# Storing the last output tiles by column halves, and the last matrix products by output block, in an encoder layer

## The chip, the cores and the metric

The kernel runs on one core of a Trainium2 chip. The metric is device time in microseconds (us). Before the change it was 1040.94 us, the median of three runs (1040.69 to 1042.45).

## The reference

One encoder layer on a 512 x 1024 float32 residual stream: a half SwiGLU step, two attention mixers with gates, and a second half SwiGLU step. Only the end of the last step bears on this change:

```python
def swiglu(h, w_in, w_out):
    gate, up = jnp.split(h @ w_in, 2, axis=-1)
    return (jax.nn.silu(gate) * up) @ w_out
...
        h = modulate(rmsnorm(x, norm_ffn2[l]), sh3, sc3)
        x = x + 0.5 * g3[:, None, :] * swiglu(h, w_ffn2_in[l], w_ffn2_out[l])
    return x
```

The returned `x` is what the kernel stores: 512 x 1024 float32, 2 MB.

## The kernel before

The stream is held transposed in eight SBUF tiles `x[0]` to `x[7]`, each 128 channels by 512 tokens (256 KB). In what follows a *row block* of the result is one such tile; its halves `T1` and `T2` are its first and last 256 tokens (`HALVES`). In DRAM the output has the same layout, `(8, 128, 512)`, so a whole tile is 128 rows of 2 KB, and one half is 128 rows of 1 KB that lie 2 KB apart.

**Units.** The second SwiGLU step is cut into units (class `Unit`), each of which makes a 2 x 2 block product with seven sub-products instead of eight. The sub-products have names: `a11`, `a12`, `s1`, `s2`, `s3`, `s4`, `a22`. An outgoing unit (`out_unit(part, g, final)`) multiplies part of `w_ffn2_out` by the activations; `g` is 0 or 1 and stands for the upper or lower four row blocks. The last two outgoing units, `end[0]` and `end[1]`, have `final=True` and `depth` 3: the operand has three slices `k` = 0, 1, 2.

**A sub-product.** `Unit.multiply(q, ks)` picks the PSUM bank and calls `two` for each `k`. A bank is 128 x 512: columns 0 to 255 are output block `j` = 0, columns 256 to 511 are block `j` = 1. For one `k`, `two` runs both blocks, and for each block three matmuls (float32 is done as high times high, high times low, low times high; lines L456, L457, L458). So a sub-product of an end unit is 3 slices x 2 blocks x 3 = 18 matmuls.

**After a sub-product.** `Unit.after(q)` adds partial results on VectorE and calls `post` when one corner of the 2 x 2 block is complete. Corner `c11` is complete after `a12`, `c22` after `s3`, `c12` after `s4` and `c21` after `a22`. In `post`, corner `c(n)(t)` updates the token half `t` of two row blocks, with one scalar-tensor-tensor instruction each (L1810): 128 x 256, `x = v * g3 + x`. The first reads columns 0 to 255 of the result, the second columns 256 to 511. For `c21`, `v` is the PSUM bank itself; for the others it is an SBUF tile.

**Stores.** In `final` units, `post` counts the updates of each tile in `seen` and stores the whole tile from SyncE's queue (SP) after its second one (L1813): tiles 0, 1, 4, 5 after `c12`, tiles 2, 3, 6, 7 after `c21`.

**Order.** The sub-products of all units stand in a list (`items`) that sets the order on TensorE. Its end is `a12`, `s2`, `s3`, `s4`, `a22`, each for `end[0]` and then for `end[1]`, so the very last 18 matmuls are `a22` of `end[1]`, into a bank of the pool `sc`; the 18 ahead of them are `a22` of `end[0]`, into a bank of `acc`. While the end units run, GpSimd's DMA queue (POOL, L511) still fetches parts of `w_ffn2_out` with an add in flight, from which the weights of `s2`, `s3` and `s4` come; these are split into high and low parts on ScalarE and VectorE (L189). SP issues its last load at about 1009 us of the span.

Of the kernel before, what the change touches and what calls it, by code (L numbers as in the profile page):

```python
# [133 lines left out]
def layer(ctx: ExitStack, tc: tile.TileContext, a: dict):  # L134
    nc = tc.nc
# [12 lines left out]
    def xt():  # L148
        return sbuf("x", [P, T], F32, 8)
# [13 lines left out]
    def bank(tag):  # L163
        return psum.tile([P, T], F32, name=name(tag), tag=tag, bufs={"acc": 3, "op": 1, "sc": 3, "tp": 1}[tag])
# [41 lines left out]
    def let_go(holder):  # L206
        for i in [i for i in holders if holders[i] == holder]:
            del holders[i]

    def load_split(src, n=1024, spare=False, aside=0):  # L210
        raw = sbuf("raw", [P, 1024], F32, RAW)
        if spare:
            hi, lo = (u4().rearrange("p a b -> p (a b)") for _ in range(2))
        else:
            hi, lo = high_low(aside=aside)
        nc.sync.dma_start(raw[:, 0:n], src)
        split_from(hi[:, 0:n], lo[:, 0:n], raw[:, 0:n])
        return hi, lo

    HALVES = (slice(0, 2 * P), slice(2 * P, T))  # L220
# [12 lines left out]
    x = [xt() for _ in range(NC)]  # L233
# [199 lines left out]
    def pair_banks():  # L433
        return (bank("acc"), bank("sc"))
# [11 lines left out]
    OPERAND = {"a11": "b11", "s1": "n1", "a12": "b21", "a22": "t4", "s4": "b22", "s2": "n2", "s3": "t3"}  # L446
    BANK = {"a11": "x", "s2": "x", "s3": "x", "a22": "x", "s1": "v", "s4": "v", "a12": "w"}
    T1, T2 = HALVES

    def two(po, w, k, x, first, last):  # L450

        (wh, wl), (xh, xl) = w, x
        for j in range(2):
            s = slice((2 * k + j) * P, (2 * k + j + 1) * P)
            out = po[:, j * H : (j + 1) * H]
            PE.matmul(out, wh[:, s], xh, start=first and j == 0, stop=False, skip_group_check=True)  # L456
            PE.matmul(out, wh[:, s], xl, start=False, stop=False, skip_group_check=True)  # L457
            PE.matmul(out, wl[:, s], xh, start=False, stop=last and j == 1, skip_group_check=True)  # L458

    class Unit:  # L460
# [12 lines left out]
        MAKE = {"s1": 5, "a11": 3, "a12": 2, "s2": 4, "s4": 2, "s3": 2, "a22": 3}  # L473
        asked, length = ("s1", "a11", "a12", "a22"), 1.0

        in_order = turned = ()
        spare, roomy, apart, more = ("s1",), (), (), {"s1": ("s2", "a11"), "s2": ("s4", "a12"), "a11": ("s3", "a21")}

        def place(self, q):
# [34 lines left out]
        def multiply(self, q, ks=None):  # L514
            b = BANK[q]
            ks = range(self.depth) if ks is None else ks
            if b not in self.bank:
                self.bank[b] = bank(self.tags.get(b) or ("sc" if self.odd else "acc"))
            po = self.bank[b]
            new = not any(BANK[d] == b for d in self.done)  # L520
            for k in ks:
                x = self.operand(OPERAND[q], k)
                two(po, self.ready[q], k, x, new and k == 0, k == self.depth - 1)
            if self.depth - 1 in ks:
                let_go((self, q))

# [96 lines left out]
    with tc.manual_schedule(engines=BOUND | {mybir.EngineType.SP, mybir.EngineType.Pool}):  # L623
# [15 lines left out]
        for n in range(NC):  # L639
            i, j = n // 4, n % 4  # L640
# [329 lines left out]
    with tc.manual_schedule(engines={mybir.EngineType.SP, mybir.EngineType.Pool}):  # L970
# [4 lines left out]
        for q in range(4, 2 * PLAIN):  # L975

            w, sums_from = loaded1, split[1]
# [4 lines left out]
            out = pair_banks()  # L982
# [14 lines left out]
        for n, chunks in enumerate(CHUNKS):  # L997


            final = n + 1 == len(CHUNKS)  # L1000
# [20 lines left out]
            out = Out1(chunks, "acc" if nxt.odd != final else "sc", final)  # L1021
            if final:
                first = range(len(chunks) - 2)
# [52 lines left out]
    for i in range(2):  # L1076
        o = ROW_LAM + 2 * i * HD
        V.tensor_tensor_reduce(
            out=lam_p[:, i, :], in0=row[:, o : o + HD], in1=row[:, o + HD : o + 2 * HD],
# [439 lines left out]
    def start_a():  # L1519
        order = [(g, i) for i in range(2) for g in range(2)]  # L1520
        ys, v = [f2() for _ in order], f2()
        nc.sync.dma_start(ys[0], qa_scr[order[0]])
        nc.sync.dma_start(v, va_scr.rearrange("p t c -> p (t c)"))
        for y, o in zip(ys[1:], order[1:]):
            banded_last[:] = [nc.sync.dma_start(y, qa_scr[o]).ins]
        mask = u4(F32).rearrange("p a b -> p (a b)")[:, 0 : 3 * P]
        nc.sync.dma_start(mask, a["mask"])
        vz = b8()
        two = [vz[:, 2 * i : 2 * i + 2, :].rearrange("p a b -> p (a b)") for i in range(2)]
        two = [v.rearrange("p (t k w d) -> p t k w d", t=NT, k=2, w=2) for v in two]  # L1530
        zero = small(1)
        V.memset(zero, 0.0)
        v4 = v.rearrange("p (t k d) -> p t k d", t=NT, k=2)
        for kv in range(2):
            for t in two:
                V.tensor_copy(t[:, :, kv, 1 - kv, :], zero.unsqueeze(1).broadcast_to([P, NT, HD]))
            split_from(*(t[:, :, kv, kv, :] for t in two), v4[:, :, kv, :])
        wa.update(mask=mask, v=two, q=(b8(), b8()), o=(b8(), b8()))
        for n, ((g, i), y) in enumerate(zip(order, ys)):
            line.at(line.now + FETCH + n, lambda g=g, i=i, y=y: turn_queries_a(g, i, y), ("tp",))  # L1540
# [178 lines left out]
    x = [xt() for _ in range(NC)]  # L1719
# [3 lines left out]
    last = []  # L1723
# [4 lines left out]
    for m in range(NC):  # L1728
        w = load_split(a["w_mix"][m], aside=MIX_ASIDES[m])
# [70 lines left out]
            yield  # L1800

    def out_unit(part, g, final):
        seen = {}

        def post(c, v, u):
            n, t = int(c[1]) - 1, int(c[2]) - 1
            for j in range(2):
                m = 4 * g + 2 * n + j
                xr = x[m][:, HALVES[t]]
                V.scalar_tensor_tensor(xr, v[:, j * H : (j + 1) * H], modv[G3][:, m : m + 1], xr, ALU.mult, ALU.add)  # L1810
                seen[m] = seen.get(m, 0) + 1
                if final and seen[m] == 2:
                    nc.sync.dma_start(a["out"][m], x[m])  # L1813

        r = slice(part.start * 2 * P, part.stop * 2 * P)
        srcs = {q: a["w2o"][g, i][:, r] for i, q in enumerate(("a11", "a12", "a21", "a22"))}
        return Unit(srcs, len(part), act_operand, post, g)
# [88 lines left out]
    with tc.manual_schedule(engines=BOUND):  # L1906
# [7 lines left out]
        for m, products in last:  # L1914
            po = bank("sc")[:, 0:H]
            run(products(po, T1))
            update(m, po, T1)
        for i, (m, products) in enumerate(last):
            po = bank("sc")[:, 0:H]
# [86 lines left out]
    for i, part in enumerate(PARTS):  # L2006
        for p in list(part)[(3 if i == 0 else 1):] + list(range(part.stop, min(part.stop + 1, NH))):
            seq.append((units[p], p - 1))
        if part.stop < NH:
            seq += [(out_unit(part, g, False), None) for g in range(2)]  # L2010

    end = [out_unit(PARTS[-1], g, True) for g in range(2)]
    for v in end:
        v.in_order = ("s4",)
    for v, p in seq:
        item(v, "s1", rest=p is None)
        item(u, "a22")
# [83 lines left out]
```

## Time and profile before

| what | value |
|---|---|
| median of the runs shown | 1040.94 us |
| span of the profiled execution, first to last instruction | 1039.1 us |
| TensorE busy (its ends are modelled) | 1031.4 us, 99% of the span |
| VectorE busy | 787.7 us, 76% |
| ScalarE busy | 583.8 us, 56% |
| granted TensorE clock, mean | 0.999 |
| share of the chain that ended last on TensorE | 94% |
| stores of the result | 8 of 256 KB, median 2.3 us from issue to landing |

The profile gives the profiled execution by its span alone; its own device time is not listed. The median of the runs shown lies 1.9 us above the span. That rest, ahead of the first and behind the last instruction, is taken as unchanged wherever a span is turned into a time.

How to read it: TensorE is busy through nearly the whole span at nearly the full clock, and the stretches without it are the start and what lies behind the last matmul. The change touches the last two units; their rows are those of the last 30 us.

### The profile page before, as it was taken

How to read it: one execution, taken by the hardware profiler on the slowest of the kernel's cores; microseconds unless marked ns; L12 is line 12 of the kernel's file. 1: busy time of each engine (PE TensorE's matmuls, PEld its weight loads, DVE VectorE, ACT ScalarE, POOL GpSimd, SP SyncE). 2: the span in 40 equal slices, each digit the busy share in tenths (PEclk: the TensorE clock that was granted, in tenths of full speed). 3: DMA queues.
4: the chain of work that ended last, by engine and by line, in shares of the span. 5: the costliest groups of instructions: out<-in, count | busy, mean ns of one | idle time of the engine just before them, and what ended most of it. 6: DMA issues, size and time to landing. Idle time of an engine off the chain costs nothing.

```text
span 1039.1 us, 18835 instructions
## 1 busy us (share of the span) xinstructions
PE 1031.4 (99%) x7346; PEld 952.4 (92%) x7346; DVE 787.7 (76%) x1456; ACT 583.8 (56%) x1014; POOL 162.9 (16%) x190
## 2 busy tenths in 40 slices
PE   9999999999999999999999999999999999999998
PEld 7789899899998998899888888989999999999998
DVE  7786667567796679859772588976899777877867
ACT  6665335244465343667785856525867546655553
POOL 1101110110110100543333101001112112212210
PEclk9999999999999999999999999999999999999999
DMA  9978787967884359796737944974498998989974
GB/s 363 358 233 203 234 231 212 257 160 221 237 203 138 146 201 410 234 286 138 182 71 190 263 129 158 359 248 102 97 237 193 246 225 207 230 221 216 206 149 112
DMA packets 69225, 220.92 MB, mean 213 GB/s; under 512 B 8336, under 2 KB 11024, under 8 KB 69136
## 3 DMA queue, kind: packets, MB, share of 16 engines
q1 hardware_dynamic: 46656, 146.52, 38.8%
q0 software_dynamic: 19344, 68.70, 36.3%
q10 hardware_dynamic: 3136, 4.51, 1.2%
q8 instruction: 57, 0.93, 0.3%
q14 instruction: 32, 0.26, 0.1%
HBM read 209.46 MB, written 10.23 MB: 211 GB/s over the span
## 4 chain that ended last, share of the span: by engine, by line
PE 94%; DMA 2%; DVE 2%; ACT 2%; issue 0%; SPq 0%; DVEq 0%; ACTq 0%
PE acc L457 7%; PE acc L456 7%; PE acc L458 7%; PE sc L456 6%; PE sc L457 6%; PE sc L458 6%; PE sc L173 5%; PE sc L174 5%; PE sc L175 5%; PE acc L173 5%; PE acc L175 5%; PE acc L174 5%; PE tp L1269 2%; DMA raw<-w1s 2%; PE acc L1193 2%; PE acc L1191 2%
## 5 line engine op out<-in xcount | busy, mean ns | idle before, releaser
L189 ACT CAST high<-raw 128x1024 fp32r<-128x1024 f32 (+2 forms) x176 | 158.4, 913 | 150.7 <-PE sc L174 41.1
L189 DVE TENSOR_TENSOR low<-raw,high 128x1024 fp32r<-128x1024 f32 (+2 forms) x176 | 183.5, 1052 | 40.2 <-ACT high L189 38.7
L456 PE MATMUL acc<-b,high 128*128 128x256 f32 x508 | 140.9, 277 | 0.0
L457 PE MATMUL acc<-b,high 128*128 128x256 f32 x508 | 140.8, 277 | 0.1
L458 PE MATMUL acc<-b,low 128*128 128x256 f32 x508 | 140.6, 277 | 0.0
L457 PE MATMUL sc<-b,high 128*128 128x256 f32 x500 | 138.2, 276 | 0.0
L456 PE MATMUL sc<-b,high 128*128 128x256 f32 x500 | 138.2, 276 | 0.0
L458 PE MATMUL sc<-b,low 128*128 128x256 f32 x500 | 138.2, 276 | 0.0
L189 ACT CAST high<-u 128x1024 fp32r<-128x1024 f32 (+1 forms) x73 | 75.5, 1035 | 52.6 <-PE sc L174 20.2
L189 DVE TENSOR_TENSOR low<-u,high 128x1024 fp32r<-128x1024 f32 (+1 forms) x73 | 87.7, 1202 | 21.3 <-ACT high L189 19.6
L173 PE MATMUL sc<-b,high 128*128 128x512 f32 (+1 forms) x272 | 97.5, 358 | 0.0
L174 PE MATMUL sc<-b,high 128*128 128x512 f32 (+1 forms) x272 | 97.1, 357 | 0.0
L175 PE MATMUL sc<-b,low 128*128 128x512 f32 (+1 forms) x272 | 97.1, 357 | 0.0
L457 PEld LDWEIGHTS acc<-b,high 128*128 128x128 f32 x508 | 95.5, 188 | 0.4 <-DVE b L1885 0.3
L456 PEld LDWEIGHTS acc<-b,high 128*128 128x128 f32 x508 | 95.5, 188 | 0.3 <-ACT f L533 0.2
L458 PEld LDWEIGHTS acc<-b,low 128*128 128x128 f32 x508 | 95.4, 188 | 0.0
L456 PEld LDWEIGHTS sc<-b,high 128*128 128x128 f32 x500 | 93.9, 188 | 0.0
L458 PEld LDWEIGHTS sc<-b,low 128*128 128x128 f32 x500 | 93.9, 188 | 0.0
L457 PEld LDWEIGHTS sc<-b,high 128*128 128x128 f32 x500 | 93.9, 188 | 0.0
L173 PE MATMUL acc<-b,high 128*128 128x512 f32 (+1 forms) x240 | 89.0, 371 | 0.0
L175 PE MATMUL acc<-b,low 128*128 128x512 f32 (+1 forms) x240 | 86.7, 361 | 0.0
L174 PE MATMUL acc<-b,high 128*128 128x512 f32 (+1 forms) x240 | 86.6, 361 | 0.0
(397 smaller groups left out, 2720.6 us busy)
## 6 DMA issues: line engine op xcount, KB each, us to landing
u<-w_mod SPq DMA_DIRECT2D x38, 512.0 KB, 8.1
b<-w_mod SPq DMA_DIRECT2D x32, 512.0 KB, 5.7
raw<-w2i SPq DMA_DIRECT2D x31, 512.0 KB, 5.4
u<-w2i POOLq DMA_DIRECT2D x31, 512.0 KB, 7.4
raw<-w1u SPq DMA_DIRECT2D x24, 512.0 KB, 6.4
u<-w1u POOLq DMA_DIRECT2D x24, 512.0 KB, 6.6
raw<-w1o SPq DMA_DIRECT2D x24, 384.0 KB, 4.9
raw<-w_gate SPq DMA_DIRECT2D x16, 512.0 KB, 5.4
```

Of the source, the lines that this page charges most:

```text
L173: PE.matmul(out, wh, xh, start=first, stop=False)
L174: PE.matmul(out, wh, xl, start=False, stop=False)
L175: PE.matmul(out, wl, xh, start=False, stop=last)
L189: last = S.copy(hi, src), V.tensor_tensor(lo, src, f(hi), ALU.subtract)
L456: PE.matmul(out, wh[:, s], xh, start=first and j == 0, stop=False, skip_group_check=True)
L457: PE.matmul(out, wh[:, s], xl, start=False, stop=False, skip_group_check=True)
L458: PE.matmul(out, wl[:, s], xh, start=False, stop=last and j == 1, skip_group_check=True)
L1191: PE.matmul(out[t][:, 0:n], hh[k][:, ht], wh[:, o : o + n], start=k == 0, stop=False)
L1193: PE.matmul(out[t][:, 0:n], hl[k][:, ht], wh[:, o : o + n], start=False, stop=k == NC - 1)
L1269: PE.transpose(tp[:, j * P : (j + 1) * P], src, ident)
```

## The change

It has two parts. (1) In a final unit each half of a tile is stored as soon as its update has been issued, in place of the whole tile after both: sixteen stores of 128 KB (128 rows of 1 KB) for eight of 256 KB. (2) In the end units the sub-product `a22` goes block by block: all three slices for columns 0 to 255, then all three for columns 256 to 511. The matmuls are the same in number and form.

```diff
-    def two(po, w, k, x, first, last):
+    def two(po, w, k, x, first, last, js=range(2)):
...
-        for j in range(2):
+        for j in js:
...
-            for k in ks:
-                x = self.operand(OPERAND[q], k)
-                two(po, self.ready[q], k, x, new and k == 0, k == self.depth - 1)
+            for js in ((0,), (1,)) if q in self.by_columns else (range(2),):
+                for k in ks:
+                    x = self.operand(OPERAND[q], k)
+                    two(po, self.ready[q], k, x, new and k == 0, k == self.depth - 1, js)
...
-        seen = {}
...
-                seen[m] = seen.get(m, 0) + 1
-                if final and seen[m] == 2:
-                    nc.sync.dma_start(a["out"][m], x[m])
+                if final:
+                    nc.sync.dma_start(a["out"][m][:, HALVES[t]], xr)
...
-        v.in_order = ("s4",)
+        v.in_order, v.by_columns = ("s4",), ("a22",)
```

In SP's queue, these are the last rows before the change: the whole tiles, named `x_872` (tile 0) to `x_879` (tile 7).

```order
L1813 DMA out<-x_872_7096 128x512 [waits DVE_49]
L1813 DMA out<-x_873_7097 128x512 [waits DMAHW1_49,DVE_49]
L1813 DMA out<-x_876_7100 128x512 [waits DMAHW2_49,DVE_49]
L1813 DMA out<-x_877_7101 128x512 [waits DMAHW3_49,DVE_49]
L1813 DMA out<-x_874_7098 128x512 [waits DVE_49]
L1813 DMA out<-x_875_7099 128x512 [waits DMAHW5_49,DVE_49]
L1813 DMA out<-x_878_7102 128x512 [waits DMAHW6_49,DMASW6_49,DVE_49]
L1813 DMA out<-x_879_7103 128x512 [waits DMAHW7_49,DVE_49]
```

With the change there are sixteen; these are the ninth to the last, the stores after `c12` and `c21`.

```order
L1811 DMA out<-x_872_7096 128x256 [waits DMAHW0_49,DVE_49]
L1811 DMA out<-x_873_7097 128x256 [waits DMAHW1_49,DVE_49]
L1811 DMA out<-x_876_7100 128x256 [waits DMAHW2_49,DVE_49]
L1811 DMA out<-x_877_7101 128x256 [waits DMAHW3_49,DVE_49]
L1811 DMA out<-x_874_7098 128x256 [waits DMAHW4_49,DVE_49]
L1811 DMA out<-x_875_7099 128x256 [waits DMAHW5_49,DVE_49]
L1811 DMA out<-x_878_7102 128x256 [waits DMAHW6_49,DVE_49]
L1811 DMA out<-x_879_7103 128x256 [waits DMAHW7_49,DVE_49]
```

The eight of the same tiles after `c11` and `c22` stand ahead of them in the same order, so half of the bytes has moved forward to the earlier updates. Each row waits for VectorE's update, and by DMAHW0 to DMAHW7 for the landing of an earlier transfer on the same of eight completion counters; for these eight rows that is the store eight places ahead.

On TensorE, these are the last nine matmuls before the change, in the `a22` of `end[1]`. The bank is `sc_1129`, and `b8_1106`, `b8_1120` and `b8_1133` hold the operand's slices `k` = 0, 1 and 2.

```order
L456 MATMUL sc_1129_11050<-b8_1120_10963,high_86 128x256
L457 MATMUL sc_1129_11050<-b8_1120_10963,high_86 128x256
L458 MATMUL sc_1129_11050<-b8_1120_10963,low_93 128x256
L456 MATMUL sc_1129_11050<-b8_1133_11106,high_86 128x256
L457 MATMUL sc_1129_11050<-b8_1133_11106,high_86 128x256
L458 MATMUL sc_1129_11050<-b8_1133_11106,low_93 128x256
L456 MATMUL sc_1129_11050<-b8_1133_11106,high_86 128x256
L457 MATMUL sc_1129_11050<-b8_1133_11106,high_86 128x256
L458 MATMUL sc_1129_11050<-b8_1133_11106,low_93 128x256
```

And these are the last nine with the change.

```order
L456 MATMUL sc_1129_11050<-b8_1106_10699,high_86 128x256
L457 MATMUL sc_1129_11050<-b8_1106_10699,high_86 128x256
L458 MATMUL sc_1129_11050<-b8_1106_10699,low_93 128x256
L456 MATMUL sc_1129_11050<-b8_1120_10963,high_86 128x256
L457 MATMUL sc_1129_11050<-b8_1120_10963,high_86 128x256
L458 MATMUL sc_1129_11050<-b8_1120_10963,low_93 128x256
L456 MATMUL sc_1129_11050<-b8_1133_11106,high_86 128x256
L457 MATMUL sc_1129_11050<-b8_1133_11106,high_86 128x256
L458 MATMUL sc_1129_11050<-b8_1133_11106,low_93 128x256
```

Before, the last six alternate between the two column blocks of one slice. Now the last nine are the three slices of the second block, and the first block is complete nine matmuls ahead of the end.

On VectorE, the last seven rows with the change are these; `acc_1126` and `sc_1129` are the two `a22` banks. Before the change the same rows stand in the same order with the same waits, the updates under L1810.

```order
L544 TENSOR_TENSOR f2_1140_11211<-f2_1140_11211,sc_1124_11015 128x512 [waits PE_49]
L1809 SCALAR_TENSOR_TENSOR x_876_7100<-f2_1140_11211,mod8_102,x_876_7100 128x256 [waits DVE_49]
L1809 SCALAR_TENSOR_TENSOR x_877_7101<-f2_1140_11211,mod8_102,x_877_7101 128x256
L1809 SCALAR_TENSOR_TENSOR x_874_7098<-acc_1126_11032,mod8_102,x_874_7098 128x256 [waits PE_49]
L1809 SCALAR_TENSOR_TENSOR x_875_7099<-acc_1126_11032,mod8_102,x_875_7099 128x256
L1809 SCALAR_TENSOR_TENSOR x_878_7102<-sc_1129_11050,mod8_102,x_878_7102 128x256 [waits PE_49]
L1809 SCALAR_TENSOR_TENSOR x_879_7103<-sc_1129_11050,mod8_102,x_879_7103 128x256
```

Of the two updates that read one bank, the first waits for TensorE and the second has no wait of its own. No row waits for a DMA.

More of the change, by code (lines that the diff above doesn't have):

```diff
@@ L474, in layer @@
         asked, length = ("s1", "a11", "a12", "a22"), 1.0
-        in_order = turned = ()
+        in_order = turned = by_columns = ()
         spare, roomy, apart, more = ("s1",), (), (), {"s1": ("s2", "a11"), "s2": ("s4", "a12"), "a11": ("s3", "a21")}
```

## The prediction

> **What bounds the kernel now.** I read the page first, for what the whole span consists of.
>
> ```profile
> span 1039.1 us, 18835 instructions
> PE 1031.4 (99%) x7346; PEld 952.4 (92%) x7346; DVE 787.7 (76%) x1456; ACT 583.8 (56%) x1014; POOL 162.9 (16%) x190
> PE 94%; DMA 2%; DVE 2%; ACT 2%; issue 0%; SPq 0%; DVEq 0%; ACTq 0%
> ```
>
> TensorE carries 94% of the chain that ended last. The change adds and removes no matmul, so it can win only behind the last one. I therefore went to the chain's end, and to VectorE and SP beside it in order of time (start, length).
>
> ```profile
> 1033.84 0.11 PE sc L457
> 1033.95 0.11 PE sc L458
> 1034.07 0.11 PE sc L456
> 1034.18 0.11 PE sc L457
> 1034.29 0.13 PE sc L458
> ```
> ```profile
> 1033.79 0.28 PE L458 MATMUL sc<-b,low 128*128 128x256 f32 x1
> 1034.13 0.28 PE L458 MATMUL sc<-b,low 128*128 128x256 f32 x1
> 1034.45 0.88 DVE L1810 SCALAR_TENSOR_TENSOR x<-sc,mod,x 128x256 f32<-128x256 f32 x2 [0.97 <-PE sc L458]
> 1030.80 4.98 SPq L1813 DMA_DIRECT2D out<-x  x8
> ```
>
> TensorE ends at 1034.41 (1034.13 + 0.28), the last two updates run from 1034.45 to 1035.33, and the span ends at 1039.1. Some 4.7 us of tail remain, and 3.7 of them lie behind the last update. What they are, the stores' own rows show: the first store alone, then the last two, and the final instructions.
>
> ```profile
> L1813 SPq DMA_DIRECT2D out<-x x1: 344/344/344, 1030.8 to 1030.8; - x1
> DMA to landing us min/median/max: 2.0/2.0/2.0
> ...
> L1813 SPq DMA_DIRECT2D out<-x x2: 332/360/387, 1035.0 to 1035.4; - x2
> DMA to landing us min/median/max: 2.2/2.5/2.8
> ```
> ```profile
> 1034.96 0.82 SPq L1813 DMA_DIRECT2D out<-x  x2
> L2096 SPq EVENT_SEMAPHORE  x12: 17/28/28, 1036.1 to 1039.0; - x12
> L2096 SPq DRAIN  x3: 7/7/7, 1038.2 to 1038.5; - x3
> ```
>
> The last store is issued at 1034.96 + 0.82 - 0.39 = 1035.39. It lands 2.8 us later, at 1038.19, which is where SP's drain stands (1038.2). What follows, 1039.07 - 1038.19 = 0.88 us, is the closing barrier. The same store with nothing ahead of it takes 2.0 us. The windows over the tail say why the last one takes longer (the last three columns: clock, DMA share, GB/s).
>
> ```profile
> 1023.50:1031.00 7.50, 7.50 (x69) 7.50 (x68) 7.21 (x13) 2.12 (x3) 0.00 (x0) 1.00 0.00 0
> 1031.60:1033.20 1.60, 1.60 (x16) 1.60 (x16) 1.57 (x5) 0.00 (x0) 0.00 (x0) 1.00 0.89 337
> 1033.20:1034.90 1.70, 1.21 (x11) 1.01 (x9) 0.73 (x3) 0.00 (x0) 0.00 (x0) 1.00 1.01 380
> 1034.90:1036.50 1.60, 0.00 (x0) 0.00 (x0) 0.42 (x2) 0.00 (x0) 0.00 (x0) 1.00 0.99 378
> ```
>
> The DMA engines idle for 7.5 us, and are then full from 1033.2 on: 2 MB at 380 GB/s want 5.5 us, and the updates give them out in 4.6 (1030.80 to 1035.39). So **the tail is bound by the DMA engines' backlog, 0.8 us at the last store** (2.8 - 2.0), on top of that store's own time.
>
> **The change, part by part.**
>
> *Half stores.* By the order, half of the bytes moves to the updates of c11 and c22. Those are done long before:
>
> ```profile
> 1018.67 0.88 DVE L1810 SCALAR_TENSOR_TENSOR x<-f,mod,x 128x256 f32<-128x256 f32 x2
> 1020.93 0.88 DVE L1810 SCALAR_TENSOR_TENSOR x<-f,mod,x 128x256 f32<-128x256 f32 x2
> 1028.78 0.88 DVE L1810 SCALAR_TENSOR_TENSOR x<-f,mod,x 128x256 f32<-128x256 f32 x2
> ```
>
> Behind 1030.8 there remain eight stores of 128 KB, 1.05 MB or 2.8 us at 380 GB/s, against 4.6 us in which they are issued. No backlog forms: -0.8 us. The last store also carries half the bytes. Each of 16 DMA engines moves 8 rows of it; a row of 2 KB and one of 1 KB cost, by the packets of a saturated window and of one that holds 1 KB rows:
>
> ```profile
> DMA packets 327, 0.60 MB, mean 378 GB/s; under 512 B 32, under 2 KB 32, under 8 KB 327
> q1 hardware_dynamic: 327, 0.60, 99.2%
> ...
> DMA packets 144, 0.13 MB, mean 94 GB/s; under 512 B 16, under 2 KB 144, under 8 KB 144
> q1 hardware_dynamic: 144, 0.13, 31.2%
> ```
>
> The first is 1034.90 to 1036.50: 0.992 x 1.6 us x 16 / 295 = 86 ns a row of 2 KB (the 32 small packets left out). The second is 618.40 to 619.80: 0.312 x 1.4 x 16 / 128 = 55 ns a row of 1 KB. So 8 rows take 0.44 us in place of 0.69: -0.25. An unhindered half store then lands in 2.0 - 0.25 = 1.75 us. No 128 KB store stands in this trace, so both ends: at best its data time halves, 2.0 - 0.34 = 1.66; at worst it lands like a 128 KB load with little beside it, from 626 to 629 us:
>
> ```profile
> q1 hardware_dynamic: 144, 0.13, 17.8%
> f<-gate_scr SPq DMA_DIRECT2D x1, 128.0 KB, 2.1
> ```
>
> I take 1.75, since a store's row (2.0 for double the bytes) is nearer than a load's. The last landing moves from 1038.19 to 1035.39 + 1.75 = 1037.14: **-1.05 us**, with ends -1.13 (1.66) and -0.70 (2.1).
>
> The page "DMA: Bandwidth & Descriptors" of the Trainium skill (Anatomy of one DMA) speaks against small stores: a fixed 2.0 us and bytes at 436 GB/s, fitted for GpSimd's path. By it 128 KB would land in 2.3 us as an estimate, and the gain would be 0.5 us. The trace has 2.0 us for 256 KB where that fit gives 2.6, so the measurement decides here.
>
> *SP's issues.* Eight more, at 0.33 to 0.39 us. They fall at 1019 to 1030, where SP has nothing else queued: nothing on the path. If that cover were gone, the last store would queue behind them, up to 0.4 us for each. The waits that are added are on stores eight places ahead; the last waits for the c22 store issued at about 1029.7 (1028.78 + 0.88), landed by 1031.8 even at 2.1 us, 3.6 us ahead of its need. Behind SP's waits only later stores are queued. SP's closing waits begin at 1036.1 and end under 1037, ahead of the new landing, so they don't become the bound.
>
> *Updates against stores in flight.* The update of one half of a tile could have waited for the store of the other half. In the order no VectorE row waits for a DMA: nothing.
>
> *Block by block.* Eighteen matmuls per unit in another order. In the chain the step inside a block (1033.84 to 1033.95 or 1034.07 to 1034.18) and the step from one block to the other (1033.95 to 1034.07) are both 0.11 to 0.12 us: the new order costs nothing, bounded by 36 x 0.01 = 0.4 us either way. What it could win is an earlier first update. But of the two updates that read a bank only the first waits for TensorE. The second needs the very last matmul and has no wait, so the first one's wait must cover the whole bank. The trace of before shows the same: block 0 was complete at 1033.79 + 0.28 = 1034.07, VectorE was idle, and the update began at 1034.45, behind the last matmul. I count 0.
>
> The page "PSUM — Partial Sum Buffer" of the Trainium skill (Terms) says why a wait would cover a bank: TensorE writing and VectorE reading the same bank and quadrant at once is an error. The trace agrees as far as it goes (1034.45 behind 1034.41); by this rule the gain of this part is nothing in any correct program.
>
> *Sum.* Span 1039.1 - 1.05 = 1038.0. The profiled execution's own time isn't listed; with the 1.87 us between its span and the median (1040.94 - 1039.07) carried over, the time is **1039.9 us**, 0.10% less.
>
> **The rivals.**
>
> *Half stores land no faster.* Completion, not data, sets the landing: 2.1 us, as the load's row has it. The backlog still goes: -0.70, **1040.2 us**. Against it: landings that grow with the queue, 2.0 to 2.8.
>
> *The first update does start early.* Then block 0's update runs during block 1's nine matmuls (9 x 0.113 = 1.0 us), and only one of the pair is left behind TensorE: 0.88 - 0.48 = 0.40 more, **1039.5 us**. Against it: the second update has no wait in the order. This is the case in which I misread the change's second part.
>
> *The early stores slow the weights* (the other side). The c11 stores, 0.5 MB, run at 1019 to 1023, when GpSimd's queue still loads the weights of s4:
>
> ```profile
> 1017.25 0.86 POOL L511 DMA_DIRECT2D u<-w2o  x1 [0.67 <-DVE low L189]
> DMA to landing us min/median/max: 5.7/5.7/5.7
> 1023.31 1.58 ACT L189 CAST high<-u 128x768 fp32r<-128x768 f32 x2
> 1025.65 0.95 DVE L189 TENSOR_TENSOR low<-u,high 128x768 fp32r<-128x768 f32 x1
> 1028.29 0.11 PE sc L456
> ```
>
> The load lands at 1017.25 + 5.7 = 1022.95. Its products begin at 1028.29, the low part is wanted by the third, at 1028.51. Cast (0.84) and subtraction (0.95) need 1.8, so it may land at 1026.7: 3.75 us to spare. The c11 stores are 1.4 us of the DMA engines at 380 GB/s. This decides only from a delay of 3.75 us, and loses on the whole from 3.75 + 1.05 = 4.8. If the load took twice its 5.7 us, TensorE would stall 5.7 - 3.75 = 1.95, and the time would be 1039.9 + 1.95 = **1041.8 us**, slower than before; by over 0.2% from a delay of 6.9 us.
>
> **How the numbers follow.** A measurement of this kernel can tell about 0.2%, 2.1 us, from no change; a gain of 1 us is under that. Chances: forecast 0.70, half stores no faster 0.16, update early 0.05, weights slowed 0.04, and 0.05 for medians moved by the runs' own scatter (1040.69 to 1042.45). The likeliest is 1039.9. All cases but the last two lie at 1039.5 to 1040.2; the range takes in the scatter downwards (0.25, and the bound of the new matmul order) and two thirds of it upwards (1.5): 1039.1 to 1041.3. Faster by over 0.2% (under 1038.86) needs twice the forecast, which no case has, and comes from scatter alone: 0.05. Slower: weights slowed beyond 6.9 us, or scatter: 0.04. Within 0.2%: 0.91.
>
> **What would show it.** Right: sixteen stores; the eight early ones in 1019 to 1030; DMA share far under 1 behind 1031; the last issue still 1.0 us behind the last matmul, landing in 1.7 to 1.8 us, all stores of the tail alike; the barrier still 0.9. The last pair of updates still begins behind the last matmul. Wrong: a first update a microsecond earlier; TensorE idle near 1026 to 1030 with its weights named; a last landing at 2.1 us or more; or a gain of over 1.5 us, which would mean that the tail held something that I haven't seen.

## The result and the profile after

The changed kernel takes 1039.97 us (median of 21 runs, 1039.54 to 1041.47), the kernel before 1041.42 us beside it (21 runs, 1040.67 to 1043.52). The ratio is 0.9986, with a 95% interval of 0.9979 to 0.9992: a gain between 0.8 and 2.2 us. The changed kernel ran twice more, beside other runs of the kernel before: 1040.64 against 1040.98 (0.9997, 0.9988 to 1.0006) and 1040.15 against 1040.95 (0.9994, 0.9985 to 1.0003). All three point the same way; only the first is clear of no change. In the profiled executions of all runs the end of the last matmul lies anywhere from 1033.9 to 1039.4 us; two traces of the changed kernel alone have it at 1034.5 and 1036.5. This scatter is larger than the terms in question, so below the *tail* is compared: from the end of the last matmul (start of its row and 0.28) to the end of the span.

First the end of TensorE and VectorE's last pair, then SP's stores and closing instructions in the changed kernel, in the views shown of before.

```profile
1034.27 0.28 PE L458 MATMUL sc<-b,low 128*128 128x256 f32 x1
1034.58 0.88 DVE L1809 SCALAR_TENSOR_TENSOR x<-sc,mod,x 128x256 f32<-128x256 f32 x2 [0.97 <-PE sc L458]
```
```profile
L1811 SPq DMA_DIRECT2D out<-x x8: 332/383/588, 1030.9 to 1035.5; - x8
DMA to landing us min/median/max: 1.7/1.8/2.0
...
L1811 SPq DMA_DIRECT2D out<-x x2: 332/358/384, 1035.1 to 1035.5; - x2
DMA to landing us min/median/max: 1.7/1.7/1.8
```
```profile
L2094 SPq DRAIN  x3: 7/7/7, 1037.4 to 1037.7; - x3
```

The last pair still begins behind the last matmul, at 1034.58 after 1034.55, with the same wait of 0.97 us. The last store is issued 0.97 us behind the matmul as before, and lands 1.77 us later in place of 2.75 (both from the trace's records). SP's drain moves up accordingly, and the span ends at 1038.20: tail 3.65 us in place of 4.66.

The stretches of the tail, with DMA share and GB/s last:

```profile
1024.50:1031.50 7.00, 7.00 (x64) 7.00 (x63) 6.96 (x13) 1.25 (x2) 0.00 (x0) 1.00 0.23 78
1031.50:1033.20 1.70, 1.70 (x17) 1.70 (x17) 1.66 (x5) 0.00 (x0) 0.00 (x0) 1.00 0.44 154
1033.20:1034.90 1.70, 1.34 (x12) 1.15 (x11) 0.73 (x3) 0.00 (x0) 0.00 (x0) 1.00 0.75 254
1034.90:1036.50 1.60, 0.00 (x0) 0.00 (x0) 0.56 (x2) 0.00 (x0) 0.00 (x0) 1.00 0.44 150
```

Where the DMA engines were full (1.01 and 0.99 of their time) they are now busy for 0.75 and 0.44 of it.

### The profile page after: what moved, and what is told of

It is laid out like the page before. It is cut to its first block, busy times and chain, and to the rows that moved or that the text cites. A ratio compares the mean times of both kernels' runs of the same rounds, so it can differ in the third digit from the quotient of the medians.

```text
span 1038.2 us, 18851 instructions
## 1 busy us (share of the span) xinstructions
PE 1030.8 (99%) x7346; PEld 951.1 (92%) x7346; DVE 786.9 (76%) x1456; ACT 583.9 (56%) x1014; POOL 162.5 (16%) x190
## 4 chain that ended last, share of the span: by engine, by line
PE 94%; DMA 2%; DVE 2%; ACT 2%; issue 0%; SPq 0%; DVEq 0%; ACTq 0%
PE acc L457 7%; PE acc L458 7%; PE acc L456 7%; PE sc L457 6%; PE sc L458 6%; PE sc L456 6%; PE sc L173 5%; PE sc L174 5%; PE sc L175 5%; PE acc L173 5%; PE acc L175 5%; PE acc L174 5%; PE tp L1270 2%; DMA raw<-w1s 2%; PE acc L1192 2%; PE acc L1194 2%
```

## The experiments

The theory was that of the prediction: the stores win about 1 us, 0.8 of it backlog and 0.25 a smaller last store; the block order wins nothing. The rivals: the block order has a part in it; smaller stores win by themselves; and part of the 0.8 is no backlog at all. In the trace of before, there is one packet of another queue, that of instructions, in the last 1.6 us of data:

```profile
q1 hardware_dynamic: 183, 0.31, 51.7%
q14 instruction: 1, 0.01, 1.2%
```

This is the view of the DMA queues of before from 1036.5 to 1038.1 (packets, MB, share of 16 engines): one packet of 8 KB, 0.31 us on one engine, at 1037.54.

All runs in one table; landings and tails are from the traces' records, in us.

| run | last store: issue behind the last matmul | its landing | tail | ratio to before (95%) |
|---|---|---|---|---|
| before | 0.99 | 2.75 | 4.66 | |
| changed kernel | 0.97 | 1.77 | 3.65 | 0.9986 (0.9979 to 0.9992) |
| halves_only | 0.97 | 1.77 | 3.65 | 0.9994 (0.9985 to 1.0003) |
| columns_only | 0.99 | 2.74 | 4.64 | 1.0007 (0.9997 to 1.0017) |
| whole_last | 0.97 | 2.68 | 4.80 | 0.9998 (0.9990 to 1.0007) |
| whole_last_rows | 0.98 | 2.28 | 4.15 | 1.0001 (0.9993 to 1.0010) |
| early_rows | 0.97 | 2.40 | 4.27 | 0.9995 (0.9987 to 1.0004) |
| late_halves | 0.97 | 1.77 | 3.65 | 0.9994 (0.9985 to 1.0003) |
| late_halves_kept | 3.99 | 1.84 | 6.74 | 1.0019 (1.0010 to 1.0028) |
| late_c11 | 0.97 | 1.77 | 3.64 | 0.9989 (0.9980 to 0.9998) |
| banks_apart | 0.55 | 1.70 | 3.15 | 0.9987 (0.9978 to 0.9995) |
| banks_again | 0.55 | 1.70 | 3.16 | 0.9987 (0.9978 to 0.9996) |
| after_again, after_third | 0.97, 0.97 | 1.76, 1.77 | 3.65, 3.66 | 0.9997 and 0.9994, as above |

**halves_only: the stores alone.**

```diff
-        v.in_order, v.by_columns = ("s4",), ("a22",)
+        v.in_order = ("s4",)
```

> The change with its stores alone; the last products in their old order. Tail = from the end of the last matmul to the end of the span: 4.66 us before the change, 3.65 with it. Theory (the whole gain comes from the stores): tail 3.65 again, last store landing 1.75 us after its issue, time 1.0 us under the kernel before. Rival (the block order has a part in it): tail longer than 3.65, up to 4.05, since 0.4 us of update would come back behind the last matmul.

Tail 3.65, landing 1.77: the theory's numbers. The time, 1040.16 against 1040.96, is 0.8 us less, which its interval doesn't separate from nothing.

**columns_only: the block order alone.** `post` is the old one, with `seen` and whole tiles.

> The change with its block order alone; whole tiles are stored as before. Theory: the first of the last two updates still begins behind the last matmul, tail 4.66, last landing 2.8 us after its issue, time as before. Rival (block order helps): the first update begins 1.0 us ahead of the last matmul's end, tail 4.26. A third view, that part of the 2.8 is an 8 KB packet of the instruction queue in the tail: SP's queue is as long as before here, so packet and 2.8 should both come again.

The last update waits as before, and tail and landing are those of before:

```profile
1036.27 0.28 PE L458 MATMUL sc<-b,low 128*128 128x256 f32 x1
1036.59 0.88 DVE L1811 SCALAR_TENSOR_TENSOR x<-sc,mod,x 128x256 f32<-128x256 f32 x2 [0.97 <-PE sc L458]
```

The last matmul ends at 1036.55 and the pair begins at 1036.59, although the first block was complete a microsecond earlier. The block order alone is worth nothing. The instruction packet is there again, 3.1 us behind the last matmul's end as before.

**early_rows: bytes as before, SP's queue as long as after.** Is the 2.75 data, or also the instruction packet? Eight small stores put as many instructions into SP's queue as the change does, and leave the 2 MB in the tail.

```diff
                 seen[m] = seen.get(m, 0) + 1
+                if final and seen[m] == 1:
+                    nc.sync.dma_start(a["out"][m][0:16, HALVES[t]], xr[0:16])
                 if final and seen[m] == 2:
                     nc.sync.dma_start(a["out"][m], x[m])
```

> Whole tiles stored as before, and in addition, at the places of the changed kernel's eight early stores, sixteen rows of each half (16 KB): SP's queue is as long as the changed kernel's, but 2 MB stay in the tail. Theory (backlog of data): last landing 2.8 us after its issue, tail 4.66, time as before. Rival (part of the 2.8 is the 8 KB packet of the instruction queue, which the changed kernel's longer SP queue moves out of the tail): packet not in the tail, last landing 2.45, tail 4.3.

The rival holds. The last two stores, and the DMA queues over 1.6 us here (1036.8 to 1038.4), to be held against the two lines of before above:

```profile
L1815 SPq DMA_DIRECT2D out<-x x2: 332/370/408, 1035.4 to 1035.9; - x2
DMA to landing us min/median/max: 2.1/2.3/2.4
```
```profile
DMA packets 216, 0.38 MB, mean 236 GB/s; under 512 B 32, under 2 KB 32, under 8 KB 216
q1 hardware_dynamic: 216, 0.38, 60.1%
```

No instruction packet, and 2.40 in place of 2.75 with the same bytes. In this run the packet stands 3.35 us ahead of the last matmul's end, in the changed kernel 3.32 ahead. So 0.36 us of the old landing came with the packet (2.752 - 2.395 in the records), and only 2.395 - 2.028 (the first, lone store) = 0.37 was backlog.

The records place the 0.36 more closely. The sixth and the seventh store, ahead of the packet, land alike in both runs (2.68 and 2.67, 2.17 and 2.13). In before, the last packet of the last store ends 0.60 us ahead of its landing, and the instruction packet lies between them, from 0.61 to 0.30 us ahead. In early_rows, as in the changed kernel, the landing follows the last packet by 0.35 to 0.36.

**whole_last: 1.5 MB in the tail.**

```diff
-                if final and seen[m] == 2:
+                if final and n == 0:
+                    nc.sync.dma_start(a["out"][m][:, HALVES[t]], xr)
+                elif final and seen[m] == 2:
                     nc.sync.dma_start(a["out"][m], x[m])
```

> Tiles 0, 1, 4 and 5 are stored in halves, tiles 2, 3, 6 and 7 whole after their second update: 1.5 MB in the tail in place of 2.0 before and 1.0 with the change. Theory (backlog 0.8 and half the bytes 0.25 are separate terms): the backlog is nearly gone, the last store waits only for the one ahead of it (issued 0.44 us earlier, 0.69 of data), so it lands 2.0 to 2.25 us after its issue; tail 3.9 to 4.15. Rival (the last stores' own size sets the landing): 2.8 and a tail of 4.66.

The theory's numbers did not come: with half a megabyte less than before, the four whole stores landed in 2.4 to 2.7 us, and the tail grew to 4.80. The landing (2.68) is near the rival's 2.8. The growth is not the landing's: from it to the end of the span it takes 1.14 us here and 0.92 before. SP's closing waits go through the eight counters in a fixed order, and with twelve stores the last one is on the fourth. Four more waits of 0.06 us each then follow its landing at 1037.54, ahead of the drain:

```profile
L2098 SPq DRAIN  x3: 7/7/7, 1037.9 to 1038.2; - x3
```

The trace also shows the instruction packet 0.1 us ahead of the last matmul's end, just where the whole stores start (DMA queues from 1033.5 to 1034.5):

```profile
q1 hardware_dynamic: 134, 0.24, 64.6%
q14 instruction: 1, 0.01, 3.6%
```

It held one of the sixteen engines for 0.036 x 1.0 x 16 = 0.58 us. From there on the stores land without a gap, 0.68, 0.68 and 0.67 us apart, and in the last store four rows follow one another at 0.08 us, one engine's pace, after all the others are done. The records don't name the engine, so that it is the one which the packet held is inferred.

**whole_last_rows: the same with the packet elsewhere.** Four more small stores at the place of c22, as in early_rows, make SP's queue as long as the changed kernel's.

> The run whole_last with four stores of sixteen rows more at the place of the c22 stores, so that SP's queue is as long as the changed kernel's. Theory (the 8 KB instruction packet comes with SP's place in its own code and, inside a saturated stretch, holds up one of the sixteen engines): packet at about 3.3 us ahead of the last matmul's end as in the changed kernel, whole last stores land 2.0 to 2.25 us after issue in place of 2.4 to 2.7, tail 3.9 to 4.15. Rival (whole stores back up by their data alone): landings and a tail of 4.8 as in whole_last.

The packet moved to 3.35 us ahead of the last matmul's end, and the last two stores landed so:

```profile
L1817 SPq DMA_DIRECT2D out<-x x2: 332/358/384, 1035.8 to 1036.2; - x2
DMA to landing us min/median/max: 2.0/2.1/2.3
```

Landing 2.28, 0.41 less than in whole_last, and a tail of 4.15, the upper end of what the theory said for both runs. (Of the 0.65 between the two tails 0.24 is the four closing waits. And whole_last issued its first two whole stores 0.3 us later against the last matmul, 0.87 and 0.43 us ahead of its end in place of 1.18 and 0.69; a part of the 0.41 may be that.) Bytes and packet are two separate terms, and the bytes ahead weigh little: with half a megabyte more in the tail, early_rows has the last landing at 2.40, 0.12 later. Its time, 1041.11 against 1040.95, shows no gain: half a microsecond of tail is lost in the scatter of the runs.

**late_halves: a miss.** Two half stores in place of the whole one, written behind a tile's second update.

> Sixteen half stores, but both halves of a tile only after its second update, so nothing moves forward. Theory: 2 MB stay in the tail and SP has to issue sixteen stores at about 0.43 us each from the first one on, 6.9 us; the last is issued some 2 us later than before and lands 1.75 to 2.0 later: tail 5.5, 0.9 us slower than before. Rival (smaller stores help by themselves): last landing sooner than 2.8 after an issue at the old place, tail 4.4.

This tested neither. A half that is complete after the first update doesn't depend on the second, and the scheduler put its store ahead: SP issued from 1020.33 on, as in the changed kernel.

```profile
1020.33 16.59 SPq L1814 DMA_DIRECT2D out<-x  x16
```

It is halves_only by another text, and gave its tail of 3.65 and a time of 1040.08.

**late_halves_kept: the same, held in program order.**

```diff
-                    nc.sync.dma_start(a["out"][m], x[m])
+                    for r in (HALVES[t], HALVES[1 - t]):
+                        tc.keep_in_program_order(nc.sync.dma_start(a["out"][m][:, r], x[m][:, r]))
```

> Sixteen half stores, both halves of a tile behind its second update, and kept in that order in SP's queue. Theory (moving bytes forward is what pays, halving alone costs): SP issues sixteen stores at about 0.43 us, 6.9 us from the first one on, and becomes the bound; the last is issued 2.9 us behind the last matmul in place of 1.0, lands 1.75 later, tail 5.5 us, 0.9 us slower than before. Rival (smaller stores help by themselves): tail under 4.66.

```profile
1030.39 8.04 SPq L1814 DMA_DIRECT2D out<-x  x16
L1814 SPq DMA_DIRECT2D out<-x x16: 332/430/484, 1030.4 to 1038.0; - x16
DMA to landing us min/median/max: 1.8/1.8/2.1
```

Right in kind, larger in size: SP is the bound. One issue follows another at (8.04 - 0.45) / 15 = 0.51 us on the average rather than 0.43; one of the steps is 0.84 long, and why the others vary from 0.39 to 0.56 is left open. The last store is issued 3.99 us behind the last matmul, the tail is 6.74, and the time is 1043.04 us, 0.19% slower than before. The last store lands sooner than before (1.84), but sixteen issues late in SP's queue lose more than that; only half stores that are issued early pay.

**after_again and after_third: the changed kernel beside the others.**

> The changed kernel itself once more, beside the three below. Tail (end of the last matmul to the end of the span) 3.65 us, last landing 1.75 to 1.8 us after its issue, time 1.0 us (0.10%) under the kernel before.

> The changed kernel again, on the same chip as the next run: tail 3.65 us, time 1.0 us under the kernel before.

Tails of 3.65 and 3.66 and landings of 1.76 and 1.77 repeat to a hundredth. The medians don't: they are 0.34 and 0.80 us under the kernel before, so a single set of runs can't weigh terms of this size, and the tails must. Taken together the sets agree with the tails: with halves_only, late_halves and late_c11, which have the same tail, six sets lie 1.45, 0.34, 0.80, 0.80, 0.88 and 1.01 us under the kernel before, 0.88 on the average against 1.01 of tail.

**late_c11: the early stores out of the way of the weights.** Each store after c11 is kept back and issued right behind one of those after c22.

> The changed kernel with the four stores after c11 put behind those after c22, past GpSimd's last loads of weights. Theory (the collision with these loads is covered by 3.75 us of slack): the second of these loads lands 5.7 us after its issue again in place of the changed kernel's later landing, and neither tail (3.65) nor time moves. Rival (the collision costs TensorE): the last matmul ends earlier against the changed kernel and the time falls by 0.1 us or more.

The second load of weights (1017.39 in the changed kernel, 1017.52 here), first in the changed kernel and then in this one:

```profile
1017.39 0.86 POOL L511 DMA_DIRECT2D u<-w2o  x1 [0.67 <-DVE low L189]
DMA to landing us min/median/max: 6.7/6.7/6.7
```
```profile
1017.52 0.86 POOL L511 DMA_DIRECT2D u<-w2o  x1 [0.67 <-DVE low L189]
DMA to landing us min/median/max: 5.8/5.8/5.8
```

Before, it was 5.7. By these rows alone the collision would cost the load 1.0 us, but they don't repeat. The same load of the changed kernel in after_again and in after_third, with the same early stores:

```profile
1019.33 0.86 POOL L511 DMA_DIRECT2D u<-w2o  x1 [0.67 <-DVE low L189]
DMA to landing us min/median/max: 5.5/5.5/5.5
```
```profile
1017.81 0.86 POOL L511 DMA_DIRECT2D u<-w2o  x1 [0.67 <-DVE low L189]
DMA to landing us min/median/max: 5.6/5.6/5.6
```

Nine traces have these c11 stores early (the three of the changed kernel, halves_only, late_halves, whole_last and whole_last_rows, banks_apart and banks_again). In three of them the load takes 6.7 to 6.9 us and in the other six 5.4 to 6.0. In the four without any (before, columns_only, late_halves_kept and this run) it takes 5.5 to 5.9. So a delay of 1 us comes in some executions alone; the early stores may cause it, but that is not shown. What repeats is the other side: the first c11 store lands only after 4.8 to 5.6 us in all nine, and after 1.7 here, issued at 1027.3. None of it reaches TensorE. It is busy for all of the 7.00 us from 1024.50 to 1031.50 in the window shown of the changed kernel, where the weights are wanted, and the tail is the same without the collision (3.64). The medians can't settle it: 1039.97 here, and 1040.64, 1039.97 and 1040.15 in the changed kernel's sets.

**banks_apart: what the block order lacked.** The two column blocks of the last unit's running sum get a PSUM bank each; the copies and the sum that read it become two of 256 columns.

```diff
+            if self.banks_apart and b == "x":
+                if "y" not in self.bank:
+                    self.bank["y"] = bank("sc" if self.odd else "acc")
+                for j in range(2):
+                    for k in ks:
+                        x = self.operand(OPERAND[q], k)
+                        one_block(self.bank["xy"[j]], self.ready[q], k, x, new and k == 0, k == self.depth - 1, j)
...
+    end[1].banks_apart = True
```

> The changed kernel with the two column blocks of the last unit's running sum in two PSUM banks, each 256 columns of its own bank, so that an update waits only for its own block. Theory (the update waits for the whole bank, and that alone keeps the block order from helping): the first of the last two updates runs beside the second block's nine matmuls, one update of 0.48 us in place of a pair of 0.88 is left behind the last matmul, tail 3.25, time 0.4 us under the changed kernel. Rival (the split costs as much): copies and sums of two halves in place of one on ScalarE and VectorE delay weights, the last matmul ends later by 0.4 us or more, and the time does not fall.

```profile
1034.43 0.48 DVE L1837 SCALAR_TENSOR_TENSOR x<-sc,mod,x 128x256 f32<-128x256 f32 x1
1035.14 0.28 PE L466 MATMUL sc<-b,low 128*128 128x256 f32 x1
1035.45 0.48 DVE L1837 SCALAR_TENSOR_TENSOR x<-sc,mod,x 128x256 f32<-128x256 f32 x1 [0.54 <-PE sc L466]
```

The pair has come apart. The first block's update runs 1.0 us ahead of the second's, beside the last matmuls, and one update is left behind them. Tail 3.15, 0.50 less than the changed kernel's (0.4 expected): 0.43 of it at the last issue, 0.07 at its landing. The rival, a later last matmul, doesn't show: it ends at 1035.42 here and 1034.81 in the second run, within the changed kernel's own 1034.55 to 1036.49.

> The run banks_apart again, beside the changed kernel on the same chip. Theory: tail 3.15 us as in its first run, time 0.5 us under the changed kernel and 1.5 us under the kernel before. Rival (its first time was scatter): no difference from the changed kernel beyond 0.2 us.

Again 3.16, and 1039.64 us against 1040.15 for the changed kernel and 1040.95 for the kernel before on the same chip: 0.5 and 1.3 us. It is the fastest version here; its lead over the changed kernel rests on two tails and two medians, not on a ratio clear of scatter.

## Why the prediction was right, and where it was not

The forecast was 1039.9 us and a gain of 1.05; measured were 1039.97, a tail shorter by 1.01, and medians lower by 1.45, 0.34 and 0.80 in three sets. That a time so near the forecast came first is in part luck: the kernel before took 1041.42 beside it, not the forecast's 1040.94, and the changed kernel's other sets gave 1040.64 and 1040.15. By its steps:

- *No matmul changes, and the win lies behind the last one.* Right: every difference that repeats is in the tail.
- *The block order counts 0.* Right, by columns_only (4.64 against 4.66) and halves_only (3.65). The reason, a wait for the whole bank, is shown by banks_apart: with a bank for each block the same order wins 0.50 us of tail. The rule of the Trainium skill's page "PSUM — Partial Sum Buffer" (Terms), that TensorE and VectorE may not use a bank's quadrant at once, agrees with both runs.
- *A half store lands in 1.75 us.* Measured 1.77, and 1.7 to 2.0 for all eight of the tail. The working was a little off both ways, and the two errors nearly cancel. A row of 1 KB takes 0.046 us and one of 2 KB 0.084 (medians in the records), so 8 rows save 0.30 and not 0.25; the first store of a pair does land in 1.70 to 1.73. The second of a pair, as the last store is, lands 0.05 later. The fit that the Trainium skill's page "DMA: Bandwidth & Descriptors" (Anatomy of one DMA) has for GpSimd's path, by which 2.3 us was estimated for 128 KB, is not what these stores of SP's queue show.
- *"-0.8 us", the backlog.* The sum was nearly right, the cause half right. This is the step that failed: "The same store with nothing ahead of it takes 2.0 us", and all the rest was put down to data. By the records the rest is 2.752 - 2.028 = 0.72, and early_rows splits it: 0.37 us of backlog, and 0.36 us that came and went with an instruction packet. Even the 0.37 is hardly the backlog of 2 MB that the prediction worked out. Half a megabyte less takes 0.12 off it (whole_last_rows); the other 0.25 stays, and the first pair of before has a like difference, 0.31, between its first and its second store (2.03 and 2.34). The change took away both terms, the packet only because eight more stores stand ahead in SP's queue. That the sum came out is luck in so far. Where the packet fell among half stores, they landed in up to 2.08 (late_halves_kept) and 2.23 us (late_c11) in place of 1.7 to 1.8. So on the last store it would have cost some 0.2 to 0.5 us of the gain, an estimate from these landings. The terms as measured: 0.36 packet, 0.37 backlog, 2.03 - 1.77 = 0.26 for half the bytes, together 2.752 - 1.773 = 0.98 of landing.
- *SP's extra issues cost nothing under cover.* Right; late_halves_kept gives the price without it, 2.1 us of tail.
- *The c11 stores and the weights.* Nothing on the path, as forecast: the load landed at most 1.2 us later than before (6.87 against 5.68), far under the point of decision, 3.75 us, and whether the stores caused even that is open.
- *Not to be told from no change.* One of three sets has an interval clear of 1, and in all three the ratio is nearer to 1 than 0.2%.

## What to carry to other kernels

Read the tail behind the last matmul as its own program: last update, issue, landing, barrier; what was stored early cost the tail nothing here, and what was only cut smaller cost an issue each (0.5 us where SP became the bound). Here, an order that was to let VectorE start on half a PSUM bank paid only with that half in a bank of its own. And before a slow landing is called backlog, look for packets of other queues among the data.

## What the runs showed of the hardware that was not expected

An 8 KB packet of the instruction queue moves with SP's instructions: 3.1 us behind the last matmul's end with eight stores, 0.1 ahead of it with twelve, 3.3 ahead with sixteen that are issued as in the changed kernel (4.3 in banks_apart). It keeps to SP's place and not to the time: with sixteen stores that are issued later it comes 1.7 us ahead (late_c11) and 2.2 us behind (late_halves_kept). In SP's recorded instructions it stands behind the 592nd to 595th in all runs with more than eight stores, and behind the 600th with eight. It holds one of the sixteen DMA engines for 0.3 to 0.8 us. With it among the last stores, the last one landed 0.36 us later (before against early_rows) and 0.41 us later (whole_last against whole_last_rows). In the changed kernel it falls between spaced stores at 1031.2, where one landed in 2.0 in place of 1.7 to 1.8 and nothing behind it was late:

```profile
q1 hardware_dynamic: 133, 0.12, 34.5%
q14 instruction: 1, 0.01, 3.7%
```

(The changed kernel's DMA queues, 1031 to 1032 us.) The page "DMA: Bandwidth & Descriptors" of the Trainium skill (Queues, rings and completion order) has queue row 14 as internal to the runtime, refills among its uses, and each engine taking turns between its rows. The rows above agree on the number of the queue and its kind; the turns themselves no row shows. That the packet is SP's own code is inferred from how it moves, and was not shown directly.
